# Merging two of the three products of a split-weight feed-forward, and spreading the conditioning steps

## Chip, core and metric

One NeuronCore of a Trainium2 chip runs the whole program; the other cores are idle. The metric is the device time of one execution in microseconds; for the kernel before, the median of three runs is 1975.13 us (1974.56 to 1978.75).

## What is computed

Two transformer blocks in a row, each of two layers, on one sequence of 256 tokens with 1024 features. All weights are fp32 and used once, so the program streams about 400 MB from HBM. The part that the change touches is the second block:

```python
cond = jax.nn.silu(c)
for l in range(DEPTH):                       # 2 layers
    mod = cond @ ada_w[l] + ada_b[l]         # 9 x 1024 values: the conditioning
    sh1, sc1, g1, sh2, sc2, g2, sh3, sc3, g3 = jnp.split(mod, N_MOD, axis=-1)
    hn = _modulate(_rms_norm(h, norm_g[l, 0]), sh1, sc1)
    h = h + 0.5 * g1[:, None, :] * _swiglu(hn, ffn1_w_in[l], ffn1_w_out[l])
    ...                                      # a mixer of four attention-like groups
    hn = _modulate(_rms_norm(h, norm_g[l, 2]), sh3, sc3)
    h = h + 0.5 * g3[:, None, :] * _swiglu(hn, ffn2_w_in[l], ffn2_w_out[l])

def _swiglu(x, w_in, w_out):                 # 1024 -> 2 x 2816 -> 1024
    gate, up = jnp.split(x @ w_in, 2, axis=-1)
    return (jax.nn.silu(gate) * up) @ w_out
```

So there are four feed-forwards, two in each layer of block 2. The conditioning is a vector times a 1024 x 9216 matrix per layer.

## The kernel before

Activations lie transposed: 128 features on the partitions, 256 tokens along the free axis, eight such tiles for 1024 features. A weight tile of 128 x 128 is the stationary operand of a TensorE product, and an activation tile of 256 columns moves past it.

**Three products per weight tile.** To keep fp32 accuracy with the fp32r format, each weight is split into a high part `wh` (a cast by ScalarE, L230) and a rest `wl` (a subtraction by VectorE, L231), and each activation into a high part `h` and a low part `l` (`hilo`, L201). `mm3` (L281) issues wh·h, wh·l and wl·h, 256 columns each, into one half of a PSUM bank; each product loads its own weights.

**Streaming.** `_plan` lists the weight chunks in order of use. `load_to` (L213) issues their DMAs on SyncE's queue, up to five sub-chunks of 128 x 1024 ahead; `split_to` (L222) splits up to three sub-chunks ahead, with four buffers each for `wh` and `wl`. `chunk` (L265) hands the tiles out and, at the start of every chunk, issues `prog["ada"]` conditioning steps. A chunk of the feed-forward is 8 x 256 columns: two sub-chunks, 16 weight tiles, 48 products.

**Conditioning.** `ada_step` (L530) does one of 144 steps: a 512 KB DMA into one of two buffers, and one VectorE multiply with a sum (L184, `ada<-ada,cond`) over 128 x 1024. `prog["ada"]` is set at L915 to L988 in block 1 and at L1082 and L1097 in `ffn`: 47 steps in each layer of block 1 (94), 24 in the first feed-forward, 26 in the second (two at each chunk from the third), none afterwards.

**Feed-forward** (`ffn`, L1065). The stage called f1 here (`gemm_shift`) multiplies the un-normalised input while the norm is computed. The stage f2 is 20 chunks; each gives one PSUM bank whose halves are gate and up. ScalarE reads the gate half and applies Silu (L1088), VectorE multiplies with the up half, and `hilo` splits the result into `hid`. The stage fd is the product with the second matrix: four groups of 256 output columns, each three chunks (8, 8 and 6 tiles deep), and after each group `gated_update` (L1049), two VectorE instructions that add the result to `x`. Names in the trace: tiles of f1 and f2 are `f`, those of fd `fd`; `hh`/`hl` and `hidh`/`hidl` are the two parts of an activation; `sg` and `sv` are the temporaries of the evacuation. Products carry L171 (`Bank.mm`), VectorE's helpers L184 to L193.

The tile framework's scheduler sets the order of the instructions on each engine's queue; every engine then works its queue in that order.

Of the kernel before, what the change touches and what calls it, by code (L numbers as in the profile page):

```python
# [121 lines left out]
def tile_model(ctx: ExitStack, tc: tile.TileContext, xT: bass.AP, pos: bass.AP, cvec: bass.AP, wst: bass.AP,  # L122
# [60 lines left out]
    def stt(out, in0, s, in1, op0, op1, **kw):  # L183
        nc.vector.scalar_tensor_tensor(out=out, in0=in0, scalar=s, in1=in1, op0=op0, op1=op1, **kw)  # L184

    def mul(out, a, b):
        tt(out=out, in0=a, in1=b, op=ALU.mult)

    def add(out, a, b):
        tt(out=out, in0=a, in1=b, op=ALU.add)  # L190
# [17 lines left out]
    for i, t in enumerate(subs):  # L208
        first_sub.setdefault(t[0], i)
    raws, split = {}, {}  # L210
    prog = {"raw": 0, "split": 0, "chunk": 0, "fill": 0, "turn": 0, "ada": 0}

    def load_to(s):  # L213
        while prog["raw"] < min(s, len(subs)):
# [50 lines left out]
    def chunk(key, l, k0, kk, c0, cc):  # L265
        j = prog["chunk"]
        assert plan[j] == (key, l, k0, kk, c0, cc), (plan[j], (key, l, k0, kk, c0, cc))
        prog["chunk"] += 1
        for _ in range(prog["ada"]):
            ada_step()  # L270
        s = first_sub[j]
        while s < len(subs) and subs[s][0] == j:
            split_to(s + 3)
            _, k, n, _, _ = subs[s]
            wh, wl = split.pop(s)
            for i in range(n):
                yield k0 + k + i, wh[:, i * cc:(i + 1) * cc], wl[:, i * cc:(i + 1) * cc]
            fill()
            s += 1
# [50 lines left out]
    def pair_outs(banks):  # L330
        return {m: (banks[m // 2], m % 2) for m in range(2 * len(banks))}
# [15 lines left out]
    def vc(n, i=0, k=1):  # L347
        return V[:, VC[n] + i:VC[n] + i + k]
# [24 lines left out]
    def sq_acc(j):  # L373
        t = t2("sq")
        act(t, xk(2 * j, 2), AF.Square)
        accumulate(0, j, t)

    class Act:
# [8 lines left out]

        def l(self, k, n=1):
            return self.lo[k // 4][:, (k % 4) * 256:(k % 4 + n) * 256]

    gfa = const([P, 8], "gfa")

# [137 lines left out]
    def ada_step():  # L530
        i = ada_n[1]
        if i >= L * 72:
            return
        ada_n[1] += 1
        ada_load(i + 2)
        l, j = i // 72, i % 72
        w = ada_raw.pop(i)
        stt(w, w, 1.0, cond[0], ALU.mult, ALU.mult, accum_out=mods[l][:, j:j + 1])
        if j == 71:
            add(mods[l], mods[l], vc(f"adab{l}", 0, 72))  # L540
            for q in range(3):
                stt(scl[l][:, 8 * q:8 * q + 8], mods[l][:, 24 * q + 8:24 * q + 16], 1.0, vc(f"ng{l}", 8 * q, 8),
                    ALU.add, ALU.mult)
                nc.vector.tensor_scalar_mul(hg[l][:, 8 * q:8 * q + 8], mods[l][:, 24 * q + 16:24 * q + 24],
                                            1.0 if q == 1 else 0.5)

    def ada_to(n):
        while ada_n[1] < n:
            ada_step()
# [69 lines left out]
    for l in range(L):  # L619
# [70 lines left out]
        def proj_pair(c, evac):  # L690
            b = Bank("pr", True)
            gemm([("A", l, 0, 8, c, 256)], h.h, h.l, pair_outs([b]), 7)
            evac(b)
# [210 lines left out]
        def gate_e(p):  # L904
            def f(b):
                s_ = th[p // 2][:, (p % 2) * 512:(p % 2) * 512 + 512]
                mul(v3(s_, 2), v3(b.t, 2), bc(rs, 2))
                if p % 4 == 3:
                    ins = act(th[p // 2], th[p // 2], AF.Tanh, scale=0.5)
                    with tc.issue_after(ins.ins):  # L910
                        ins = act(th[p // 2 - 1], th[p // 2 - 1], AF.Tanh, scale=0.5)
                    base_table(ins)
            return f

        prog["ada"] = 1  # L915
        for p in range(12):
            proj_pair(4352 + 256 * p, gate_e(p))

        prog["ada"] = 0
        mixed = [u4("mx") for _ in range(2)]  # L920
        mh = Act(8, "mh")
        for n, (y, gg) in enumerate(((ya, ga), (yb, gb), (yc, gc))):
# [45 lines left out]
        def hid_e(b, m):  # L968
# [3 lines left out]
            mul(q_, r_, r_)  # L972
            sub(hid.l(m, 2), q_, hid.h(m, 2).bitcast(F32))

        b4 = [Bank("u1", True) for _ in range(4)]
        gemm([("U", l, 2 * i, 2, 0, 1024) for i in range(4)], h.h, h.l, pair_outs(b4), 7, after={1: nrm2})
        for j in range(4):
# [2 lines left out]
        bd = [Bank("dn", True) for _ in range(4)]  # L980
        for half in range(2):
            for i in (range(4, 8) if half == 0 else range(8, 16)):
                prog["ada"] = min(2, i - 4)
                b = Bank("u2", half == 0)
                gemm([("U", l, 0, 8, 256 * i, 256)], h.h, h.l, pair_outs([b]), 7)
                hid_e(b, 2 * i)
            for m in range(4):
                prog["ada"] = 0 if half and m == 3 else 1  # L988
                gemm([("D", l, 8 * k, 8, 256 * m, 256) for k in (2 * half, 2 * half + 1)], hid.h, hid.l,
                     pair_outs([bd[m]]), 31)  # L990
                if half and l == 0:
                    update(m, bd[m], "full", rsm, "mix1", nh)
                elif half:
                    if m == 0:
                        ada_to(72)
                        mul(gfa, vc("final", 0, 8), scl[0][:, 0:8])
                        xa = Shifted(0, 0, lambda k: gfa[:, k:k + 1])
                    update(m, bd[m], "full", rsm)
                    xa.parts(m)
                    dst = t2("sqf")  # L1000
                    for e in range(2):
                        act(dst[:, e * 256:(e + 1) * 256], xk(2 * m + e), AF.Square, scale=vc("final", 2 * m + e))
                    accumulate(1, m, dst)
# [39 lines left out]
    def following(l, i):  # L1043
        l, i = (l, i + 1) if i < 2 else (l + 1, 0)
        if l == L:
            return None
        return Shifted(l, i, lambda k: scl[l][:, 8 * i + k:8 * i + k + 1])

    def gated_update(j, bank, l, i, nxt, part=None):  # L1049
        for e in range(2) if part is None else (part,):  # L1050
            k = 2 * j + e
            stt(xk(k), bank.t[:, e * 256:(e + 1) * 256], hg[l][:, 8 * i + k:8 * i + k + 1], xk(k), ALU.mult, ALU.add)
            if nxt is None:
                nc.sync.dma_start(outT[:, k * 256:(k + 1) * 256], xk(k))
        if nxt is None:
            return
        sq_acc(j)
        nxt.parts(j)

# [3 lines left out]
        return b  # L1063

    def ffn(l, f, i, xa, first=False):  # L1065
        h, r = Act(8, "h"), rcomb if first else rsx
        hid = Act(22, "hid")
        b4 = [Bank("f1", True) for _ in range(4)]
        nrm = normalised(h, l, i, first)
        gemm_shift(("F" + f, l, 0, 8, 0, 512), xa, b4, lambda: next(nrm))  # L1070
        for j in range(2):
            s_, q_ = t1("sg"), t1("sv")
            bg_, bu_ = b4[2 * j], b4[2 * j + 1]
            cg, cu = shift_bias(bg_), shift_bias(bu_)
            mul(s_, bg_.t[:, 0:256], r)
            act(s_, s_, AF.Silu, bias=cg)
            mul(q_, bu_.t[:, 0:256], r)
            stt(q_, q_, cu, s_, ALU.add, ALU.mult)
            hilo(q_, hid.h(j), hid.l(j))
        for j in range(20):  # L1080
            if j == 2:
                prog["ada"] = 1 if first else 2  # L1082
            if first and j in range(2, 10):
                next(nrm)
            b = Bank("f2", True)
            gemm([("F" + f, l, 0, 8, 512 + 256 * j, 256)], h.h, h.l, pair_outs([b]), 7)
            s_, q_ = t1("sg"), t1("sv")
            ins = act(s_, b.t[:, 0:256], AF.Silu)  # L1088
            mul(q_, s_, b.t[:, 256:512])
            hilo(q_, hid.h(j + 2), hid.l(j + 2))  # L1090
        if i == 2:
            ada_to(L * 72)
        nxt = following(l, i)
        base_table(ins)
        for m in range(4):
            if m == 2:
                prog["ada"] = 0  # L1097
            b = Bank("fd", True)
            parts = [("G" + f, l, k, kk, 256 * m, 256) for k, kk in ((0, 8), (8, 8), (16, 6))]
            if nxt is None and m == 3:  # L1100
                gemm(parts[:2], hid.h, hid.l, pair_outs([b]), 21)
                parts = list(chunk(*parts[2]))
                for e in range(2):
                    for k, wh, wl in parts:
                        mm3(b, b.t[:, e * 256:e * 256 + 256], wh[:, e * P:(e + 1) * P], wl[:, e * P:(e + 1) * P],
                            hid.h(k), hid.l(k), k == 21)
                    gated_update(m, b, l, i, nxt, e)
            else:
                gemm(parts, hid.h, hid.l, pair_outs([b]), 21)
                gated_update(m, b, l, i, nxt)  # L1110
        return nxt
# [411 lines left out]
```

## Time and profile before

| What | Value |
|---|---|
| median of 3 runs | 1975.13 us (1974.56 to 1978.75) |
| profiled execution, its own time | 1979.56 us |
| its span, first to last instruction | 1977.8 us |
| PE busy, DVE busy, ACT busy | 1950.8, 1465.2, 1084.9 us |
| products (MATMUL) | 15554 |
| HBM read | 402.96 MB, 204 GB/s over the span |
| mean granted TensorE clock | 0.991 |

The profiled execution lies 4.4 us above the median of the runs; the span is 1.8 us shorter than the execution. Products are pipelined: a product's duration in the trace (283 ns for 256 columns) is its latency, and what a stream of them costs is the distance from one start to the next.

### The profile page before, as it was taken

What the parts mean: (1) busy time and instruction counts of PE and PEld (TensorE: products, weight loads), DVE (VectorE), ACT (ScalarE), POOL (GpSimd) and SP (SyncE); (2) the same over time, 40 slices, a digit from 0 to 9 for tenths busy, and PEclk for the clock granted to TensorE, in tenths of its full rate; (3) what the DMA queues carried; (4) which work ended last, traced back from release to release, by engine and by line L of the source; (5) the groups of instructions that cost most, each with busy time, mean ns of one, the idle gap of its engine ahead of it and who ended that gap; (6) DMA issues with size and microseconds to landing.
All of it is one profiled execution on the core that took longest, in us unless ns stands there. A gap on an engine that the chain in (4) does not pass through costs nothing.

```text
span 1977.8 us, 38149 instructions
## 1 busy us (share of the span) xinstructions
PE 1950.8 (99%) x15554; PEld 1883.1 (95%) x15554; DVE 1465.2 (74%) x2243; ACT 1084.9 (55%) x1654; POOL 86.3 (4%) x86
## 2 busy tenths in 40 slices
PE   8999999999999999999999999999999999999999
PEld 7989999999999999999999997999999999889999
DVE  7878778696677786789877698788565557977553
ACT  5756545354565555445644467744464446576442
POOL 1000010001000010002000000000000000000000
PEclk9999999999999999999999998999999999999999
DMA  7545656896444655888577643388556555334554
GB/s 257 178 154 202 219 183 244 303 322 234 155 150 167 229 186 187 304 318 293 200 283 265 222 145 117 108 304 313 189 166 211 183 176 167 121 126 162 182 173 126
DMA packets 114945, 406.51 MB, mean 206 GB/s; under 512 B 12880, under 2 KB 14672, under 8 KB 114768
## 3 DMA queue, kind: packets, MB, share of 16 engines
q1 hardware_dynamic: 114768, 404.06, 59.8%
q8 instruction: 122, 2.00, 0.4%
q14 instruction: 55, 0.45, 0.1%
HBM read 402.96 MB, written 1.05 MB: 204 GB/s over the span
## 4 chain that ended last, share of the span: by engine, by line
PE 87%; DVE 6%; ACT 3%; DMA 2%; issue 1%; SPq 0%; POOL 0%; POOLq 0%; DVEq 0%; ACTq 0%
PE f L171 23%; PE fd L171 13%; PE pr L171 12%; PE dn L171 9%; PE u L171 9%; PE br L171 3%; PE wo L171 2%; PE mo L171 2%; DVE wl L231 2%; PE a L171 2%; DVE cv L184 1%; DMA raw<-wst_dram 1%; PE sbv L171 1%; PE rv L171 1%; PE uq L171 1%
## 5 line engine op out<-in xcount | busy, mean ns | idle before, releaser
L230 ACT CAST wh<-raw 128x1024 fp32r<-128x1024 f32 (+1 forms) x627 | 643.5, 1030 | 679.5 <-PE fd L171 119.8
L231 DVE TENSOR_TENSOR wl<-raw,wh 128x1024 fp32r<-128x1024 f32 (+1 forms) x627 | 756.0, 1210 | 330.0 <-ACT wh L230 329.0
L171 PE MATMUL f<-hh,wl 128*128 128x256 f32 x1280 | 363.8, 284 | 2.0 <-DVE wl L231 1.8
L171 PE MATMUL f<-hh,wh 128*128 128x256 f32 x1280 | 363.1, 284 | 0.8 <-ACT wh L230 0.8
L171 PE MATMUL f<-hl,wh 128*128 128x256 f32 x1280 | 363.0, 284 | 0.6 <-DVE hl L193 0.6
L171 PEld LDWEIGHTS f<-hh,wl 128*128 128x128 f32 x1280 | 246.4, 193 | 3.6 <-DVE wl L231 3.6
L171 PEld LDWEIGHTS f<-hh,wh 128*128 128x128 f32 x1280 | 246.4, 193 | 1.1 <-ACT wh L230 1.0
L171 PEld LDWEIGHTS f<-hl,wh 128*128 128x128 f32 x1280 | 246.4, 192 | 0.8 <-DVE hl L193 0.8
L184 DVE SCALAR_TENSOR_TENSOR ada<-ada,cond 128x1024 f32<-128x1024 f32 x144 | 176.5, 1227 | 59.5 <-DMA ada<-ada_dram 58.9
L171 PE MATMUL fd<-hidh,wh 128*128 128x256 f32 x704 | 199.3, 283 | 0.6 <-DVE x L184 0.6
L171 PE MATMUL fd<-hidl,wh 128*128 128x256 f32 x704 | 199.2, 283 | 0.0
L171 PE MATMUL fd<-hidh,wl 128*128 128x256 f32 x704 | 199.2, 283 | 0.0
L171 PE MATMUL pr<-hh,wh 128*128 128x256 f32 x672 | 194.8, 290 | 0.0
L171 PE MATMUL pr<-hl,wh 128*128 128x256 f32 x672 | 190.0, 283 | 0.0
L171 PE MATMUL pr<-hh,wl 128*128 128x256 f32 x672 | 190.0, 283 | 0.0
L171 PE MATMUL u<-hh,wh 128*128 128x256 f32 x512 | 145.3, 284 | 0.0
L171 PE MATMUL dn<-hidh,wh 128*128 128x256 f32 x512 | 144.9, 283 | 0.0
L171 PE MATMUL dn<-hidl,wh 128*128 128x256 f32 x512 | 144.9, 283 | 0.0
L171 PE MATMUL dn<-hidh,wl 128*128 128x256 f32 x512 | 144.9, 283 | 0.0
L171 PE MATMUL u<-hh,wl 128*128 128x256 f32 x512 | 144.9, 283 | 0.0
L171 PE MATMUL u<-hl,wh 128*128 128x256 f32 x512 | 144.9, 283 | 0.0
L171 PEld LDWEIGHTS fd<-hidh,wh 128*128 128x128 f32 x704 | 135.2, 192 | 0.8 <-DVE x L184 0.8
(476 smaller groups left out, 4478.1 us busy)
## 6 DMA issues: line engine op xcount, KB each, us to landing
raw<-wst_dram SPq DMA_DIRECT2D x599, 512.0 KB, 3.8
ada<-ada_dram SPq DMA_DIRECT2D x144, 512.0 KB, 5.1
raw<-wst_dram SPq DMA_DIRECT2D x22, 256.0 KB, 2.7
raw<-wst_dram SPq DMA_DIRECT2D x4, 390.0 KB, 3.0
R<-ret_dram SPq DMA_DIRECT2D x2, 512.0 KB, 7.6
out_dram<-x SPq DMA_DIRECT2D x8, 128.0 KB, 4.0
C<-cst_dram SPq DMA_DIRECT2D x1, 896.0 KB, 7.2
v<-vec_dram SPq DMA_DIRECT2D x2, 448.0 KB, 5.0
```

The costliest lines, as they stand in the source:

```text
L171: nc.tensor.matmul(out, lhsT=lhsT, rhs=rhs, start=grp not in self.open, stop=stop, skip_group_check=True)
L184: nc.vector.scalar_tensor_tensor(out=out, in0=in0, scalar=s, in1=in1, op0=op0, op1=op1, **kw)
L230: nc.scalar.copy(wh[:, :n * cc], src)
L231: ins = tt(out=wl[:, :n * cc], in0=src, in1=wh[:, :n * cc].bitcast(F32), op=ALU.subtract)
```

## The change

In the four feed-forwards the activation pair is laid out so that the high and low part of a tile stand in one buffer, 512 columns apart (`Pair`), and `hl(k)` is one operand of two strips of 256 columns. `gemm_ab` issues, for each weight tile, one product wh·(h and l) of 512 columns over a whole PSUM bank and one product wl·h of 256 columns into the bank's first half. An output tile of 128 x 256 so takes a whole bank, whose halves have to be added: in f2 by a ScalarE copy and a VectorE add for gate and for up, in fd (the first three of the four groups) by two updates of `x` instead of one. f1 and the fourth group of fd keep `mm3`. The conditioning steps are counted in fractions per chunk: 0.5 in the first up-projection chunks, 1 in the later stages of the first block, 0.7 in f2 and 1 in the first three groups of fd, until all 144 are done; each third of a layer's modulation vector is finished as soon as its 24 steps are.

```diff
-        for _ in range(prog["ada"]):
+        prog["due"] += prog["ada"]
+        while prog["due"] >= 1.0:
+            prog["due"] -= 1.0
             ada_step()
...
+    class Pair(Act):
+        def __init__(self, n, s):
+            self.t = [u4(s, dt=F32R) for _ in range((n + 1) // 2)]
+        def h(self, k, n=1):
+            return self.t[k // 2][:, (k % 2) * 256:(k % 2 + n) * 256]
+        def l(self, k, n=1):
+            return self.t[k // 2][:, 512 + (k % 2) * 256:512 + (k % 2 + n) * 256]
+        def hl(self, k):
+            return v3(self.t[k // 2], 2)[:, :, (k % 2) * 256:(k % 2) * 256 + 256]
+
+    def gemm_ab(chunks, a, banks, klast):
+        for c in chunks:
+            for k, wh, wl in chunk(*c):
+                for m, b in enumerate(banks):
+                    b.mm(v3(b.t, 2), wh[:, m * P:(m + 1) * P], a.hl(k), stop=False)
+                    b.mm(b.t[:, 0:256], wl[:, m * P:(m + 1) * P], a.h(k), stop=k == klast)
...
-        if j == 71:
-            add(mods[l], mods[l], vc(f"adab{l}", 0, 72))
...
+        if j % 24 == 23:
+            q = j // 24
+            mq = mods[l][:, 24 * q:24 * q + 24]
+            add(mq, mq, vc(f"adab{l}", 24 * q, 24))
...
+        prog["ada"] = 0.5
         b4 = [Bank("u1", True) for _ in range(4)]
...
-                prog["ada"] = min(2, i - 4)
+                prog["ada"] = 1
...
+    def gated_update_ab(j, banks, l, i, nxt):
+        for e in range(2):
+            k = 2 * j + e
+            for c in range(2):
+                stt(xk(k), banks[e].t[:, c * 256:(c + 1) * 256], hg[l][:, 8 * i + k:8 * i + k + 1], xk(k), ALU.mult,
+                    ALU.add)
...
     def ffn(l, f, i, xa, first=False):
-        h, r = Act(8, "h"), rcomb if first else rsx
-        hid = Act(22, "hid")
+        h, r = Pair(8, "h"), rcomb if first else rsx
+        hid = Pair(22, "hid")
...
         for j in range(20):
-            if j == 2:
-                prog["ada"] = 1 if first else 2
+            prog["ada"] = 0.7
...
-            b = Bank("f2", True)
-            gemm([("F" + f, l, 0, 8, 512 + 256 * j, 256)], h.h, h.l, pair_outs([b]), 7)
+            bb = [Bank("f2", True) for _ in range(2)]
+            gemm_ab([("F" + f, l, 0, 8, 512 + 256 * j, 256)], h, bb, 7)
             s_, q_ = t1("sg"), t1("sv")
-            ins = act(s_, b.t[:, 0:256], AF.Silu)
-            mul(q_, s_, b.t[:, 256:512])
+            for t_, b in zip((s_, q_), bb):
+                nc.scalar.copy(t_, b.t[:, 256:512])
+                add(t_, b.t[:, 0:256], t_)
+            ins = act(s_, s_, AF.Silu)
+            mul(q_, s_, q_)
             hilo(q_, hid.h(j + 2), hid.l(j + 2))
-        if i == 2:
-            ada_to(L * 72)
...
         for m in range(4):
-            if m == 2:
-                prog["ada"] = 0
+            prog["ada"] = 1 if m < 3 else 0
+            parts = [("G" + f, l, k, kk, 256 * m, 256) for k, kk in ((0, 8), (8, 8), (16, 6))]
+            if m < 3:
+                bb = [Bank("fd", True) for _ in range(2)]
+                gemm_ab(parts, hid, bb, 21)
+                gated_update_ab(m, bb, l, i, nxt)
+                continue
```

What the scheduler makes of it shows on three queues in f2 of the second feed-forward. TensorE before, from the last tile of one pair of sub-chunk buffers (`wh_15479`, `wl_15480`) to the first of the next; the chunk's bank is `f_2405`:

```order
L171 MATMUL f_2405_15543<-hh_14992,wh_15479 128x256
L171 MATMUL f_2405_15543<-hl_14994,wh_15479 128x256
L171 MATMUL f_2405_15543<-hh_14992,wl_15480 128x256
L171 MATMUL f_2405_15543<-hh_14993,wh_15509 128x256
L171 MATMUL f_2405_15543<-hl_14995,wh_15509 128x256
L171 MATMUL f_2405_15543<-hh_14993,wl_15510 128x256
```

Every weight tile makes three products of 256 columns. And now, over four weight tiles; the chunk has a bank for gate, `f_2477`, and one for up, `f_2478`:

```order
L171 MATMUL f_2477_15442<-h_14605,wh_15390 128x512
L171 MATMUL f_2477_15442<-h_14605,wl_15391 128x256
L171 MATMUL f_2478_15443<-h_14605,wh_15390 128x512
L171 MATMUL f_2478_15443<-h_14605,wl_15391 128x256
L171 MATMUL f_2477_15442<-h_14606,wh_15390 128x512
L171 MATMUL f_2477_15442<-h_14606,wl_15391 128x256
L171 MATMUL f_2478_15443<-h_14606,wh_15390 128x512
L171 MATMUL f_2478_15443<-h_14606,wl_15391 128x256
```

Two products of 256 columns have become one of 512, and the third stays. VectorE in the same stage, before: one chunk's evacuation and two conditioning steps (`wl_15656` is used two chunks after `f_2405`, `wl_15699` three chunks after it).

```order
L187 TENSOR_TENSOR sv_15611<-sg_15610,f_2405_15543 128x256
L231 TENSOR_TENSOR wl_15656<-raw_15507,wh_15655 128x1024
L193 TENSOR_TENSOR hidl_15003<-sv_15611,hidh_14997 128x256
L231 TENSOR_TENSOR wl_15699<-raw_15550,wh_15698 128x1024
L184 SCALAR_TENSOR_TENSOR ada_15617,mods_161<-ada_15617,cond_1820 128x1024
L184 SCALAR_TENSOR_TENSOR ada_15620,mods_161<-ada_15620,cond_1820 128x1024
```

Both splits and two conditioning steps stand behind the multiply that waits for the chunk's last product. And now, from a chunk that has a conditioning step ahead of it to the next chunk's first add (`wl_15531` is used two chunks after `f_2477`, `wl_15565` three chunks after it):

```order
L184 SCALAR_TENSOR_TENSOR ada_15503,mods_161<-ada_15503,cond_1820 128x1024
L190 TENSOR_TENSOR sg_15491<-f_2477_15442,sg_15491 128x256
L231 TENSOR_TENSOR wl_15531<-raw_15410,wh_15530 128x1024
L190 TENSOR_TENSOR sv_15492<-f_2478_15443,sv_15492 128x256
L187 TENSOR_TENSOR sv_15492<-sg_15491,sv_15492 128x256
L231 TENSOR_TENSOR wl_15565<-raw_15447,wh_15564 128x1024
L193 TENSOR_TENSOR hid_14615<-sv_15492,hid_14615 128x256
L190 TENSOR_TENSOR sg_15550<-f_2488_15501,sg_15550 128x256
```

The weight splits keep their lead in the queue; two adds came in, and at most one conditioning step stands in a chunk instead of two. ScalarE for the same chunk, now:

```order
L1128 COPY sg_15491<-f_2477_15442 128x256
L230 CAST wh_15530<-raw_15410 128x1024
L1128 COPY sv_15492<-f_2478_15443 128x256
L1130 ACTIVATE sg_15491<-sg_15491 128x256
L230 CAST wh_15564<-raw_15447 128x1024
L202 CAST hid_14615<-sv_15492 128x256
```

Two copies came in, and the two casts of weights stand between the steps of the evacuation. The conditioning steps on VectorE's queue are now 80 in block 1, 23 in the first feed-forward, 23 in the second and 18 in the third.

## Rows read from the trace of the kernel before

**Rows 1.** Page, head and parts 1 and 2: busy time, share, count; granted clock in tenths.
```profile
span 1977.8 us, 38149 instructions
...
PE 1950.8 (99%) x15554; PEld 1883.1 (95%) x15554; DVE 1465.2 (74%) x2243; ACT 1084.9 (55%) x1654; POOL 86.3 (4%) x86
...
PEclk9999999999999999999999998999999999999999
```
**Rows 2.** Page, part 4: chain that ended last, by engine and by line.
```profile
PE 87%; DVE 6%; ACT 3%; DMA 2%; issue 1%; SPq 0%; POOL 0%; POOLq 0%; DVEq 0%; ACTq 0%
PE f L171 23%; PE fd L171 13%; PE pr L171 12%; PE dn L171 9%; PE u L171 9%; PE br L171 3%; PE wo L171 2%; PE mo L171 2%; DVE wl L231 2%; PE a L171 2%; DVE cv L184 1%; DMA raw<-wst_dram 1%; PE sbv L171 1%; PE rv L171 1%; PE uq L171 1%
```
**Rows 3.** Chain in time, first feed-forward: start us, us, what, count.
```profile
966.68 109.45 PE f L171 x910
1076.13 61.81 PE fd L171 x515
```
**Rows 4.** PE timeline, first mixer, 512-column products: start us, us, what.
```profile
1210.61 0.39 PE L171 MATMUL mv<-wh,hh 128*128 128x512 f32 x1
...
1216.06 0.39 PE L171 MATMUL mv<-wh,hl 128*128 128x512 f32 x1
```
**Rows 5.** PE timeline, block 1, 512-column products just after an interruption.
```profile
66.40 0.40 PE L171 MATMUL sbv<-wh,hl 128*128 128x512 f32 x1
...
68.71 0.39 PE L171 MATMUL sbv<-wl,hh 128*128 128x512 f32 x1
```
**Rows 6.** Tile f, f2 of feed-forwards 1, 2, 3: count, ns, first and last start us.
```profile
L171 PE MATMUL f<-hh,wh x320: 280/283/386, 959.0 to 1075.6; 128*128 128x256 f32 x160
...
L171 PE MATMUL f<-hh,wh x320: 280/283/415, 1279.0 to 1399.2; 128*128 128x256 f32 x160
...
L171 PE MATMUL f<-hh,wh x320: 280/283/283, 1475.7 to 1590.8; 128*128 128x256 f32 x160
```
**Rows 7.** Windows: us, PE, PEld, DVE, ACT, POOL busy, clock, DMA share, GB/s.
```profile
1279.00:1399.50 120.50, 118.18 (x962) 116.96 (x961) 96.00 (x152) 58.26 (x90) 0.00 (x0) 0.99 0.81 282
1363.90:1367.30 3.40, 3.40 (x18) 3.40 (x18) 3.40 (x7) 0.89 (x2) 0.00 (x0) 0.50 0.85 304
1475.70:1591.20 115.50, 115.46 (x963) 115.26 (x962) 68.49 (x94) 58.37 (x90) 0.00 (x0) 1.00 0.54 181
```
**Rows 8.** Waits of DVE, 1279 to 1399.5 us.
```profile
DVE ada L184 <- DMA ada<-ada_dram: 8.5, 10, 2.0
```
**Rows 9.** Waits of PE, whole program: us in total, times, longest.
```profile
PE f L171 <- DVE wl L231: 1.8, 4, 0.8
```
**Rows 10.** Page, part 5: busy us, mean ns, idle before.
```profile
L230 ACT CAST wh<-raw 128x1024 fp32r<-128x1024 f32 (+1 forms) x627 | 643.5, 1030 | 679.5 <-PE fd L171 119.8
L231 DVE TENSOR_TENSOR wl<-raw,wh 128x1024 fp32r<-128x1024 f32 (+1 forms) x627 | 756.0, 1210 | 330.0 <-ACT wh L230 329.0
...
L184 DVE SCALAR_TENSOR_TENSOR ada<-ada,cond 128x1024 f32<-128x1024 f32 x144 | 176.5, 1227 | 59.5 <-DMA ada<-ada_dram 58.9
```
**Rows 11.** Tiles f, fd, hidl, vn: ns least/median/most, first and last start.
```profile
L1088 ACT ACTIVATE sg<-f x80: 368/380/386, 966.2 to 1911.0; 128x256 f32<-128x256 f32 x80
L187 DVE TENSOR_TENSOR sv<-sg,f x80: 410/414/417, 968.0 to 1912.3; 128x256 f32<-128x256 f32 x80
...
L193 DVE TENSOR_TENSOR hidl<-sv,hidh x88: 414/424/429, 964.3 to 1913.2; 128x256 fp32r<-128x256 f32 x88
...
L1303 ACT COPY vn<-gv x4: 368/380/392, 1189.5 to 1705.2; 128x256 f32<-128x256 f32 x4
...
L184 DVE SCALAR_TENSOR_TENSOR x<-fd,hg,x x32: 472/476/484, 1093.4 to 1974.3; 128x256 f32<-128x256 f32 x32
```
**Rows 12.** DVE and ACT timelines, f2 of feed-forward 3, one evacuation.
```profile
1502.26 0.42 DVE L193 TENSOR_TENSOR hidl<-sv,hidh 128x256 fp32r<-128x256 f32 x1 [0.47 <-ACT hidh L202]
1503.21 1.23 DVE L231 TENSOR_TENSOR wl<-raw,wh 128x1024 fp32r<-128x1024 f32 x1 [0.53 <-ACT wh L230]
...
1501.82 0.41 ACT L202 CAST hidh<-sv 128x256 fp32r<-128x256 f32 x1 [1.34 <-DVE sv L187]
```

More of the change, by code (lines that the diff above doesn't have):

```diff
@@ L210, in tile_model @@
     raws, split = {}, {}
-    prog = {"raw": 0, "split": 0, "chunk": 0, "fill": 0, "turn": 0, "ada": 0}
+    prog = {"raw": 0, "split": 0, "chunk": 0, "fill": 0, "turn": 0, "ada": 0.0, "due": 0.0}
     def load_to(s):
@@ L538, in ada_step @@
         stt(w, w, 1.0, cond[0], ALU.mult, ALU.mult, accum_out=mods[l][:, j:j + 1])
-        if j == 71:
-            add(mods[l], mods[l], vc(f"adab{l}", 0, 72))
[L541 to L545, printed above, removed]
+        if j % 24 == 23:
+            q = j // 24
+            mq = mods[l][:, 24 * q:24 * q + 24]
+            add(mq, mq, vc(f"adab{l}", 24 * q, 24))
+            stt(scl[l][:, 8 * q:8 * q + 8], mq[:, 8:16], 1.0, vc(f"ng{l}", 8 * q, 8), ALU.add, ALU.mult)
+            nc.vector.tensor_scalar_mul(hg[l][:, 8 * q:8 * q + 8], mq[:, 16:24], 1.0 if q == 1 else 0.5)
     def ada_to(n):
@@ L994, in tile_model @@
                     if m == 0:
-                        ada_to(72)
+                        ada_to(24)
                         mul(gfa, vc("final", 0, 8), scl[0][:, 0:8])
@@ L1046, in following @@
             return None
+        ada_to(72 * l + 24 * (i + 1))
         return Shifted(l, i, lambda k: scl[l][:, 8 * i + k:8 * i + k + 1])
@@ L1056, in gated_update, with take_up @@
             return
+        take_up(j, nxt)
+    def gated_update_ab(j, banks, l, i, nxt):
[4 more added lines that the diff above has]
+                    ALU.add)
+            if nxt is None:
+                nc.sync.dma_start(outT[:, k * 256:(k + 1) * 256], xk(k))
+        if nxt is not None:
+            take_up(j, nxt)
+    def take_up(j, nxt):
         sq_acc(j)
@@ L1095, in ffn @@
         for m in range(4):
-            if m == 2:
-                prog["ada"] = 0
+            prog["ada"] = 1 if m < 3 else 0
[5 more added lines that the diff above has]
+                continue
             b = Bank("fd", True)
-            parts = [("G" + f, l, k, kk, 256 * m, 256) for k, kk in ((0, 8), (8, 8), (16, 6))]
             if nxt is None and m == 3:
```

## The prediction, made before the run

> **What bounds the kernel now.** I read the page first, then the chain, then TensorE's timeline inside the feed-forwards. TensorE (PE) is busy 99% of the span at the full clock in nearly every slice [rows 1], and the chain runs through it for 87%, 36% in the feed-forwards' tiles f and fd alone [rows 2]. So a feed-forward costs what its stream of products costs. That is the distance between starts, not the 283 ns of a product: in the first feed-forward 515 fd products follow each other in 61.81 us, 120.02 ns each, with nothing between them [rows 3].
>
> A product of 512 columns is in the trace too, in the mixer: 24 steps from 1210.61 to 1216.06 us, 227.1 ns each [rows 4]. So 256 more columns cost 107.1 ns, and about 13 ns of a product does not depend on its columns. Two merged products save that part once. Just behind an interruption the same kind of product runs at 231 ns (10 steps in 2.31 us, [rows 5]).
>
> Then f2 of the feed-forwards side by side. The third takes 115.1 us from its first to its last wh·h product, the first 116.6, the second 120.2 [rows 6]. The second is the one with two conditioning steps per chunk: it moves 282 GB/s against 181, VectorE (DVE) is busy 96.0 us against 68.5 [rows 7], and DVE stands 8.5 us there waiting for conditioning DMAs [rows 8]. PE waits for weight splits [rows 9], and after those waits the granted clock is 0.50, the 1.2 GHz level, for 3.4 us [rows 7]. So 5.1 us of that stage are not products.
>
> **The products.** f2 has 20 chunks of 16 weight tiles, 320; three groups of fd have 3 x 22 x 2 = 132. Over four feed-forwards 1808 weight tiles change from three products to two. Before, a tile costs 3 x 120.02 = 360.06 ns; after, 227.1 + 120.02 = 347.1. Saved: 1808 x 12.9 = 23.4 us.
>
> No row shows a product whose moving operand is two strips, as `hl(k)` is. Bounds: 227.1 if the strips stream as one [rows 4], 240.04 if the second costs as much as a product of its own [rows 3], thus 23.4 us down to 0. I take 227.1: the feed-forward's stream is as unbroken as the mixer's. At the 231 of rows 5 it would be 1808 x 9.0 = 16.3 us; that is the low end of my own case. Below 227.1 I do not go, because those rows already hold one weight load per product.
>
> The Trainium skill speaks against this sum: "TensorE: Matmul & The Clock Gate", section "Back-to-back issue gap", gives the isolated gap as N / 2.4 + 2.5 ns, so a merged pair would save 2.5 ns, an estimate of 4.5 us over the 1808 tiles in place of 23.4. The trace does not agree: by that formula 256 columns cost 109 ns, and rows 3 have 120.02.
>
> **The evacuation.** f2 adds two ScalarE (ACT) copies (0.38 us by the nearest PSUM copy) and two DVE adds per chunk (0.41 us, the multiply that reads PSUM now) [rows 11]. A chunk now lasts 16 x 347.1 = 5.55 us on PE. DVE's own work in it: two splits at 1.21, four small operations at 0.41 and 0.7 steps at 1.23 [rows 10, 11], 2.42 + 1.64 + 0.86 = 4.92 us; 5.29 in a chunk with a step. ACT: two casts at 1.03, two copies, Silu and the split cast, about 0.4 each: 3.6 us. Both fit, but a queue is worked in order, so I lay the queues out from the end t = 0 of a chunk's products. ACT: copy to 0.38, cast to 1.41, copy to 1.79, Silu to 2.17; the second cast needs a buffer that PE leaves half a chunk later, at 2.78, and ends at 3.81, the split cast [rows 12] at 4.22. DVE: add to 0.79, split from 1.41 to 2.62, add to 3.03, multiply to 3.44, split from 3.81 to 5.02, subtract to 5.43, conditioning step to 6.66. The next chunk's copy is there at 5.55 + 0.38 = 5.93, so its add starts 0.7 us late, at 6.66. That does not pile up: its second split cannot start before that chunk's 3.81 anyway, and the operations ahead of it still end by then. The splits made here belong to the chunks two and three further on; the first is done at 2.6 and used at 5.55 + 2.78 = 8.3 us. So PE waits for neither: cost nothing, hidden by products. Without that lead every microsecond of lateness is PE's.
>
> At the start of a feed-forward the cover is thin: the normalisation is still in DVE's queue when f2 begins, and the first f2 loses about 1.5 us against the third [rows 6]. Two more adds there are at most 0.82 us in each of four, 3.3 us; at the other end nothing. I take 1 us, since most of the queue there is ACT's.
>
> The two extra updates of x (0.48 us each, [rows 11]) in three groups of fd lie under the next group's 15 us of products: nothing. Without that cover they would cost 4 x 3 x 0.95 = 11 us.
>
> **The conditioning steps.** Still 144. Block 1 has 80 instead of 94, the feed-forwards 23, 23, 18 and 0 instead of 24, 26, 0, 0. Each is 1.23 us of DVE and a 512 KB DMA on SP's queue, among the weight loads. In the second feed-forward at most one step per chunk asks for 1.05 + 0.7 x 0.52 = 1.41 MB in 5.55 us, 255 GB/s, where two asked for 2.10 MB in 5.76, 364 GB/s; 304 were moved in its worst stretch [rows 7]. So the DMA waits, the PE waits and the clock drop go: 5.1 us back, at least none. In fd a step per chunk asks for (1.05 + 0.52) / 5.55 = 283 GB/s, 315 in the short third chunk: about the measured flow, carried by the weights loaded ahead. In the third feed-forward 18 steps fall where DVE has room (68.5 of 115.5 us, [rows 7]). The few small instructions that now finish each third of a modulation vector: nothing, there are six lots of them.
>
> **The sum.** 23.4 + 5.1 - 1.0 = 27.5 us. The profiled execution takes 1979.56 us (span 1977.8) and would take 1952.1; it lies 4.4 us over the median of the runs, 1975.13, so for the median I forecast 1947.6 us. A measurement here can tell about 0.2%, 4 us, from no change.
>
> **Rivals.** *A: DVE is late now and then.* All feed-forwards with steps behave like the second one now, which loses 5.1 us over its 13 chunks with steps, 0.39 each; the 42 f2 chunks with a step would lose 16.4 us: 1964. For it: DVE is fuller than today, 4.92 of 5.55 us. Against it: that stage lost its time with DMA waits [rows 8], which the spreading takes away.
>
> *B: the merged product costs what two cost, 240.04 ns*, because a second strip starts anew. Then only the conditioning gains: 1947.6 + 23.4 = 1971. Against it: rows 4, though with one strip. The skill's 2.5 ns would land near this case, an estimate of 1966.5.
>
> *C: the handovers set the period, slower.* DVE has waits of 0.47 and 0.53 us for ACT inside one evacuation today [rows 12]. If they stay and the new add waits 0.38 for its copy, a chunk with a step takes 5.29 + 0.47 + 0.53 + 0.38 = 6.67 us, 1.12 over PE's 5.55; 42 of them cost 47 us: 1994.6. It ends slower than today as soon as such a chunk passes 5.55 + 27.5 / 42 = 6.20 us. For it: strict order on both queues. Against it: in the new order splits stand in the places where those waits were, and the lead of two chunks.
>
> **How the numbers follow.** Forecast 0.81, A 0.09, B 0.05, C 0.05. My own case runs from 16.3 + 2.5 - 3.3 = 15.5 us saved (half of the 5.1 kept) to 28.5; that is 1960 to 1946.6. The range takes in A at its upper end and the 2 to 4 us by which runs differ: 1943.5 to 1964.5. Faster: the forecast, A and half of B, which ends at the bound of 4 us, 0.925; the rest of B is no change, C slower. Rounded 0.92, 0.03 and 0.05.
>
> **What would show it.** In f2 and fd the starts should alternate in steps of 227 and 120 ns, and f2 should take about 111 us in the second to fourth feed-forward alike, 112 in the first. PE's waits for weight splits and the half clock at 1364 us should be gone, and the half clocks in the mixers stay. DVE should be busy about 102 us in an f2 with steps. It is wrong if the wide product steps at 235 ns or more, or if PE waits for `wl` in every chunk.

## The result, and the profile after

The changed kernel takes 1957.12 us (median of 4 runs, 1951.53 to 1960.48) against 1975.55 (4 runs, 1974.56 to 1978.75): a ratio of 0.9907, interval 0.9892 to 0.9922, so 18.4 us gained. The forecast was 1947.6 us, with 27.5 us gained; 1957.1 lies inside its range. The profiled execution is the slowest of the four.

The head of the page, its granted clock and its chain, to be read against [rows 1, 2]: there are 1808 products fewer (13746 instead of 15554), and TensorE (PE) is still the bound.

```profile
span 1958.6 us, 34892 instructions
...
PE 1932.8 (99%) x13746; PEld 1782.3 (91%) x13746; DVE 1531.2 (78%) x2431; ACT 1134.3 (58%) x1814; POOL 85.1 (4%) x86
...
PEclk9999999999999999999999999899999999999999
...
PE 88%; DVE 7%; ACT 3%; issue 1%; DMA 0%; POOL 0%; SPq 0%; POOLq 0%; DVEq 0%; ACTq 0%
```

Did the evacuation stay hidden? PE's waits in the whole program, for the feed-forwards' tile f:

```profile
PE f L171 <- DVE h L193: 0.9, 1, 0.9
```

There is one wait, at the start of a feed-forward (the kernel before has one of 0.6 us there); the wait for `wl` of [rows 9] is gone. The windows of f2 in feed-forwards 1 to 4, against [rows 7] (us, then PE, PEld, DVE, ACT, POOL busy, clock, DMA share, GB/s):

```profile
958.80:1073.40 114.60, 113.53 (x641) 97.90 (x641) 99.36 (x169) 71.73 (x131) 0.00 (x0) 1.00 0.72 250
1276.60:1389.70 113.10, 113.10 (x642) 98.09 (x641) 96.57 (x163) 71.25 (x129) 0.00 (x0) 1.00 0.72 250
1465.00:1576.20 111.20, 111.20 (x642) 96.97 (x641) 95.74 (x162) 70.94 (x129) 0.00 (x0) 1.00 0.73 254
1778.40:1891.60 113.20, 113.20 (x642) 97.98 (x641) 82.67 (x130) 69.15 (x126) 0.00 (x0) 1.00 0.57 185
```

The clock is full in all four, PE has no gap in the last three, VectorE (DVE) has 15 to 31 us left. Yet the third takes 111.2 us and the second and fourth take 2 us more, with as many products, no wait, and in the fourth less DVE work and less traffic. So the products themselves are spaced differently. PE's timeline in the second (start us, busy us, what), from one wide product to the one 30 weight tiles on:

```profile
1300.31 0.40 PE L171 MATMUL f<-h,wh 128*128 128x512 f32 x1
1300.56 0.28 PE L171 MATMUL f<-h,wl 128*128 128x256 f32 x1
1300.67 0.40 PE L171 MATMUL f<-h,wh 128*128 128x512 f32 x1
1300.91 0.28 PE L171 MATMUL f<-h,wl 128*128 128x256 f32 x1
...
1310.91 0.40 PE L171 MATMUL f<-h,wh 128*128 128x512 f32 x1
```

and the same in the third:

```profile
1500.32 0.39 PE L171 MATMUL f<-h,wh 128*128 128x512 f32 x1
1500.55 0.27 PE L171 MATMUL f<-h,wl 128*128 128x256 f32 x1
1500.66 0.40 PE L171 MATMUL f<-h,wh 128*128 128x512 f32 x1
1500.89 0.28 PE L171 MATMUL f<-h,wl 128*128 128x256 f32 x1
...
1510.72 0.39 PE L171 MATMUL f<-h,wh 128*128 128x512 f32 x1
```

10.60 us / 30 = 353.3 ns per weight tile, and 10.40 / 30 = 346.7. The slow rhythm repeats after three tiles: wide and narrow steps of 233 + 117, 241 + 120 and 236 + 113 ns. The fast one has wide steps of 231 to 233 ns and narrow ones of 112 to 118.

Neither rhythm changes in the middle of an undisturbed stream. In this trace f2 of the second to fourth feed-forward has one irregular place each, 4 to 6 us after its start; what is ahead of it may run in the other rhythm, and what is behind it keeps its rhythm to the end of the merged part of fd. The third feed-forward, which counts as fast, began slowly (x2 is two products in one row):

```profile
1465.00 0.39 PE L171 MATMUL f<-h,wh 128*128 128x512 f32 x1
...
1470.65 0.64 PE L171 MATMUL f<-h,wh 128*128 128x512 f32 x2
...
1471.54 0.40 PE L171 MATMUL f<-h,wh 128*128 128x512 f32 x1
```

The first 16 tiles took 5.65 us, 353.1 ns each; the next two took 0.89 us instead of 0.7, and from there the stream is fast. What the irregular place is stays open.

A feed-forward has 452 merged tiles, so the two rhythms lie 452 x 6.67 = 3.01 us apart; against the 360.0 ns of before one saves 3.01 us and the other 6.03. Here feed-forwards 1, 2 and 4 were slow and 3 was fast: 3 x 3.01 + 6.03 = 15.1 us.

### The profile page after: what moved, and what is told of

The parts are those of the page before. It is cut to its first block, busy times and chain, and to the rows that moved or that the text cites. A ratio compares the mean times of both kernels' runs of the same rounds, so it can differ in the third digit from the quotient of the medians.

```text
span 1958.6 us, 34892 instructions
## 1 busy us (share of the span) xinstructions
PE 1932.8 (99%) x13746; PEld 1782.3 (91%) x13746; DVE 1531.2 (78%) x2431; ACT 1134.3 (58%) x1814; POOL 85.1 (4%) x86
## 4 chain that ended last, share of the span: by engine, by line
PE 88%; DVE 7%; ACT 3%; issue 1%; DMA 0%; POOL 0%; SPq 0%; POOLq 0%; DVEq 0%; ACTq 0%
PE f L171 24%; PE fd L171 13%; PE pr L171 13%; PE dn L171 9%; PE u L171 9%; PE br L171 4%; PE wo L171 2%; PE mo L171 2%; DVE wl L231 2%; DVE cv L184 2%; PE a L171 2%; PE sbv L171 1%; PE rv L171 1%; PE uq L171 1%; PE z L171 1%
## 5 line engine op out<-in xcount | busy, mean ns | idle before, releaser
L171 PE MATMUL f<-h,wh 128*128 128x512 f32 x1280 | 450.3, 398 | 0.9 <-DVE h L193 0.9
L171 PE MATMUL f<-h,wl 128*128 128x256 f32 x1280 | 358.0, 280 | 0.1
L171 PEld LDWEIGHTS f<-h,wh 128*128 128x128 f32 x1280 | 240.1, 188 | 59.7 <-DVE h L193 1.3
L171 PE MATMUL fd<-hid,wh 128*128 128x512 f32 (+1 forms) x880 | 249.3, 352 | 0.6 <-DVE x L184 0.6
L171 PEld LDWEIGHTS f<-h,wl 128*128 128x128 f32 x1280 | 241.2, 189 | 1.3 <-DVE wl L231 1.3
L171 PE MATMUL fd<-hid,wl 128*128 128x256 f32 x704 | 197.6, 281 | 0.0
L171 PEld LDWEIGHTS fd<-hid,wh 128*128 128x128 f32 x880 | 154.0, 189 | 25.2 <-DVE x L184 0.8
L171 PEld LDWEIGHTS fd<-hid,wl 128*128 128x128 f32 x704 | 133.4, 189 | 0.0
L171 PEld LDWEIGHTS pr<-hh,wh 128*128 128x128 f32 x672 | 128.7, 191 | 3.7 <-issue 2.3
L171 PEld LDWEIGHTS pr<-hl,wh 128*128 128x128 f32 x672 | 128.8, 192 | 1.1 <-issue 1.0
```

The lines of the kernel that those rows point to most:

```text
L171: nc.tensor.matmul(out, lhsT=lhsT, rhs=rhs, start=grp not in self.open, stop=stop, skip_group_check=True)
```

## The experiments

**Three questions at once: which part brings the gain, does the rhythm stay at its places, what makes it.** The change once more; each half of the change alone; and the product stretches alone.

`after_again`: the change, unaltered.

> The changed kernel as it is, a second trace. In the first one a weight tile's pair of products costs 353.3 ns in feed-forwards 1, 2 and 4 and 346.7 in feed-forward 3, each value steady for over 140 us. Rhythm theory: these are two rhythms that the stream of products keeps up by itself, and what ran just ahead decides which; then a feed-forward can change its value from one execution to the next, and the time with it by about 452 tiles x 6.6 ns = 3.0 us each. Place theory (rival): the value hangs on where the buffers of a feed-forward lie; then the same three have 353.3 again and the third 346.7. Time by both 1951 to 1961 us.

`ada_only`: the kernel before, three products, with the conditioning steps spread as in the change.

```diff
-        for _ in range(prog["ada"]):
+        prog["due"] += prog["ada"]
+        while prog["due"] >= 1.0:
+            prog["due"] -= 1.0
             ada_step()
...
+            prog["ada"] = 0.7
...
+            prog["ada"] = 1 if m < 3 else 0
```

> The kernel before with the conditioning steps spread as in the change, and three products per weight tile as before. My sum gave the spreading 5.1 us: f2 of the second feed-forward falls from 120.2 to about 115.1 us, PE's waits there and the half clock at 1364 us go, the rest stays: about 1970.4 us, ratio 0.9974. Rival: the steps that moved into the third feed-forward and into fd cost there what they no longer cost in the second; then no change, 1975.

`ab_only`: the change with the steps placed as before.

```diff
-            prog["ada"] = 0.7
+            if j == 2:
+                prog["ada"] = 1 if first else 2
...
+        if i == 2:
+            ada_to(L * 72)
...
```

> The changed kernel with the conditioning steps placed as before the change. If the two parts of the change only add up, the products alone give what the trace of the change shows for them, three feed-forwards x 452 x 6.8 + one x 452 x 13.4 = 15.3 us: 1960 us, and f2 of the second feed-forward is 5 us longer than that of the fourth. Rival: with the two more adds VectorE can't carry two steps per chunk, 2.42 + 1.64 + 2.46 = 6.52 us against 5.6 of products, so 13 chunks lose about 0.9 us each, 12 us in that stage: 1967 us.

`micro`: no model, only stretches of 128 weight tiles on the same kinds of buffers, each opened by a wait of PE for DVE and then by a number of short products ("kicks"), so that a stretch meets its first product in another way.

```python
...
for p in range(NPAIR):      # order "ab", strips or one strip
    a(p)                    # wh, 512 columns
    c(p, p >= fin)          # wl, 256 columns
...
```

> No part of the model is computed: the output is the input x. One set of buffers, stretches of 128 tiles each behind a wait of PE for VectorE: alternating 512 and 256 columns (two strips) with 0, 1, 2, 3 and 5 products of 128 columns ahead; 512 alone; 256 alone; alternating with one strip of 512; 256 first; two wide then two narrow; four wide then four narrow; three of 256. Rhythm theory: the alternating stretches fall into two values, 353 and 347 ns per tile, by what is ahead of them, with one strip as with two; 512 alone settles at 227, 256 alone at 120, groups of four near 347. Place theory: all alternating stretches of two strips have one value. Strip theory (second rival): one strip costs 347 always, two strips 353.

Measured, the kernel before taking 1974.9 us beside them: `after_again` 1956.17 (ratio 0.9904, 0.9887 to 0.9921), `ada_only` 1976.0 (1.0002, 0.9988 to 1.0016), `ab_only` 1960.85 (0.9911, 0.9882 to 0.9940). The products alone bring about 14 of the 18.7 us, with intervals that overlap; spreading alone brings nothing that can be told, at most 2.4 us by its interval. So the gain comes from the products, and what the spreading adds to them is taken up below. f2 of the second and fourth feed-forward in `after_again` (count, ns least/median/most, first and last start):

```profile
L171 PE MATMUL f<-h,wh x320: 392/395/499, 1277.2 to 1388.0; 128*128 128x512 f32 x160
...
L171 PE MATMUL f<-h,wh x320: 387/398/403, 1776.4 to 1889.3; 128*128 128x512 f32 x160
```

The second, slow in the first trace of the same program, is now fast (110.8 us, against 353.3 x 319 = 112.7); the fourth is slow. So the rhythm is not tied to the place in the program or its buffers.

`micro` (740.09 us) gives the prices without the model, each a stretch of equal products (start, length to the last modelled end, count):

```profile
219.62 5.60 PE L54 MATMUL wide<-h,wh 128*128 128x512 f32 x24
...
246.74 4.48 PE L54 MATMUL nar<-h,wl 128*128 128x256 f32 x36
```

23 steps in 5.60 - 0.39 us are 226.5 ns, and this is the form with two strips; with one strip [rows 4] have 227.1. 35 steps in 4.48 - 0.28 us are 120.0. Rival B falls: a second strip costs nothing. Three narrow products per tile cost 360.0 ns, as in the kernel before. Alternated, wide and narrow products ran at 346.7 ns per tile behind no kick and at 353.3 behind 1, 2, 3 and 5; twice 346.7 with one strip; 353.3 both times when the narrow one came first. Wide, wide, narrow, narrow gave 348.3 both times it was run. Four wide and four narrow, expected near 347, gave 350.0 behind no kick and 350.8 behind two.

**Are the two strips the cause?** In `micro` one strip had been fast twice. `whole` stores both parts of an activation tile side by side, so that the moving operand is one strip of 512; `whole_ab_only` adds the old placing of the steps to that; `micro2` runs strips and one strip behind 0 to 5 kicks and behind 6 to 9 narrow products; `before_again` is the kernel before, traced once more.

```diff
...
         def hl(self, k):
-            return v3(self.t[k // 2], 2)[:, :, (k % 2) * 256:(k % 2) * 256 + 256]
+            return self.t[k // 2][:, (k % 2) * 512:(k % 2) * 512 + 512]
...
-                    b.mm(v3(b.t, 2), wh[:, m * P:(m + 1) * P], a.hl(k), stop=False)
+                    b.mm(b.t, wh[:, m * P:(m + 1) * P], a.hl(k), stop=False)
...
```

> The changed kernel with the high and low part of an activation tile side by side, so that the moving operand of the wide product is one strip of 512 columns. In the stretches measured by themselves one strip ran at 346.7 ns per tile twice out of two, two strips at 346.7 once and at 353.3 four times. If one strip keeps the stream in the faster rhythm, all four feed-forwards show 346.7: f2 near 111 us in each but the first (112.5), 1808 x 6.6 = 11.9 us less than a changed kernel with all four slow, 9 us less than the first trace: 1948 us, and less spread between executions than the 9 us of the change. Rival: one strip had luck twice; then the feed-forwards are mixed again and the time is that of the change, 1956.

> The same with the conditioning steps placed as before the change, two per chunk in the second feed-forward. With the rhythm out of play it tells what the spreading is worth beside the merged products. If VectorE can't carry two steps and two more adds, that f2 loses 5 us or more against the one of the run named whole, as it did in the trace of the products alone (117.7 against 113.1): 1953 us. Rival: the loss shows in profiled executions only, and the times of the two agree within 2 us.

> No part of the model is computed: the output is the input x. Stretches of 128 tiles, alternating 512 and 256 columns, two strips and one strip in turn on the same buffers, behind 0 to 5 products of 128 columns or 6 to 9 products of 256 columns. Strip theory in its weaker form: one strip always ends in the rhythm of 346.7 ns, two strips in either. Rival: both layouts show both values.

> The kernel before, a second trace. In the first one f2 of the second feed-forward took 120.2 us, 5.1 more than the third, and 37 us of the whole ran at half clock. The spreading alone brought nothing in the times, 1976.0 against 1974.9 us. Theory: the 5 us belong to that one execution, and a second trace shows less of them. Rival: they are there again, and the spreading pays as much elsewhere, in the third feed-forward and the mixers.

Measured, the kernel before taking 1974.91 us: `whole` 1951.13 us (0.9883, 0.9866 to 0.9899), `whole_ab_only` 1961.08 (0.9930, 0.9917 to 0.9944). `micro2` (984.42 us), two stretches with strips (`str`) and two with one strip (`one`), behind 0 and 1 kicks, each pair of lines the start and, 12 tiles on, the end of a measurement:

```profile
29.64 0.39 PE L53 MATMUL str<-h,wh 128*128 128x512 f32 x1
...
33.80 0.39 PE L53 MATMUL str<-h,wh 128*128 128x512 f32 x1
...
79.95 0.39 PE L53 MATMUL one<-h,wh 128*128 128x512 f32 x1
...
84.11 0.39 PE L53 MATMUL one<-h,wh 128*128 128x512 f32 x1
...
124.61 0.40 PE L53 MATMUL str<-h,wh 128*128 128x512 f32 x1
...
128.85 0.40 PE L53 MATMUL str<-h,wh 128*128 128x512 f32 x1
...
169.63 0.40 PE L53 MATMUL one<-h,wh 128*128 128x512 f32 x1
...
173.87 0.40 PE L53 MATMUL one<-h,wh 128*128 128x512 f32 x1
```

4.16 / 12 = 346.7 and 4.24 / 12 = 353.3, each with strips and with one strip. One strip was fast behind 0, 3 and 5 kicks and slow behind 1, 2 and 4; strips were slow behind 1 and 4 only. Behind 6 to 9 narrow products strips were fast once (6) and one strip was fast once (9). So the strips are not the cause. Nor does the number of kicks fix the rhythm: strips behind 2, 3 and 5 were slow in `micro` and fast here. In the trace of `whole` itself the first feed-forward is fast as far as the middle of fd, and the second to fourth are slow:

```profile
L171 PE MATMUL f<-h,wh x320: 387/398/458, 1271.5 to 1384.2; 128*128 128x512 f32 x160
```

112.7 us, as in the change. Why `whole` nonetheless has the lowest median here is open. Its interval overlaps the change's, and its runs had a high granted clock, a mean of 0.995 to 0.997 where those of the kernel `grouped` below have 0.993 to 0.995.

`before_again` (1973.52 us) tests the 5.1 us that the prediction saw lost to DMA waits in the second feed-forward. Its f2 there, and its window:

```profile
L171 PE MATMUL f<-hh,wh x320: 280/283/284, 1280.4 to 1395.8; 128*128 128x256 f32 x160
```

```profile
1280.40:1396.10 115.70, 115.66 (x962) 115.29 (x961) 95.77 (x152) 58.76 (x90) 0.00 (x0) 1.00 0.83 294
```

115.4 us against 120.2 in [rows 6], clock 1.00, PE with no gap, DVE as busy as in [rows 7]. DVE waits 5.2 us for conditioning there and PE loses nothing by it. So the loss was an incident of the one execution that the prediction read; how often it comes is not known.

With merged products it is another matter. `ab_only` in the same stretch, window and waits of PE:

```profile
1275.90:1393.60 117.70, 114.99 (x642) 97.59 (x641) 106.58 (x186) 70.75 (x129) 0.00 (x0) 1.00 0.81 289
```

```profile
PE f L171 <- DVE wl L231: 2.0, 4, 0.8
PE f L171 <- ACT wh L230: 0.6, 1, 0.6
```

Two steps per chunk beside the new adds make DVE 106.6 us busy of 117.7, and PE waits for splits: f2 takes 117.7 us where the change's first trace has 113.1, 4.6 more, although its rhythm changes about the places where PE waits and a fifth of its tiles ran fast. By whole times, spreading is worth 10 us in the form with one strip (1961.08 against 1951.13, intervals apart) and 4.7 in the form with strips (1960.85 against 1956.17, intervals overlapping). The stretch shows 2.7 us of the ten (f2 of `whole_ab_only` 115.7 us against 113.0). The granted clock goes with part of the rest (mean 0.993 to 0.997 over its runs, 0.995 to 0.997 over those of `whole`). In the traces it is lower in the two mixers (0.95 and 0.95, from 1150 to 1265 and from 1650 to 1770 us, against 0.97 and 0.99), where neither kernel has a conditioning step. So part of the ten may not be the spreading's at all; this is not settled.

**Can the order take the rhythm away?** `grouped` runs, for each activation tile, both wide products and then both narrow ones. `micro3` runs four orders (wide wide narrow narrow; wide narrow narrow wide; two wide, four narrow, two wide; eight and eight), each behind 0, 1, 2 and 4 kicks. `after_third` is the change a third time. `grouped_all` also merges the fourth group of fd where another feed-forward follows.

```diff
                 for m, b in enumerate(banks):
                     b.mm(v3(b.t, 2), wh[:, m * P:(m + 1) * P], a.hl(k), stop=False)
+                for m, b in enumerate(banks):
                     b.mm(b.t[:, 0:256], wl[:, m * P:(m + 1) * P], a.h(k), stop=k == klast)
```

```diff
-            if m < 3:
+            if m < 3 or nxt is not None:
                 bb = [Bank("fd", True) for _ in range(2)]
```

> The changed kernel with the four products of a gate and an up tile in the order wide, wide, narrow, narrow. Measured by itself this order gave one value behind two different beginnings, 348.3 ns per tile. If that holds in the kernel, all four feed-forwards show 348.3: f2 near 111.5 us in the second to fourth and 113 in the first, 1808 x 11.8 = 21.3 us less products than before: 1953.6 us by the median 1974.9, and 9 us less than a changed kernel with four slow feed-forwards. Rival: the steady value is disturbed in the kernel by the waits at each chunk and the time is that of the change, 1956.5.

> No part of the model is computed: the output is the input x. Stretches of 128 tiles behind 0, 1, 2 and 4 products of 128 columns, in four orders of wide (a) and narrow (b) products: aabb, abba, aabbbbaa and eight a then eight b. If long runs of equal products are what settles, eight and eight come closest to 226.7 + 120 = 346.7 whatever is ahead; abba and aabbbbaa have no value yet. Rival: every order has a fast and a slow rhythm, and none is free of what is ahead of it.

> The changed kernel as it is, beside the run named grouped_all on the same chip, and a third trace. By the rhythm theory each of its four feed-forwards shows 346.7 or 353.3 ns per tile, mostly the slow one as so far (5 of 8), and the time scatters by more than the grouped order does: median 1956, range 8 us or more. Rival: the slow value is tied to feed-forwards 1 and 4, which had it in both traces.

> The grouped order (wide, wide, narrow, narrow), also in the fourth group of fd in the first three feed-forwards: 3 x 44 tiles go from 360.1 to 348.3 ns, 1.6 us. But the two updates of x more that this adds (0.95 us) stand at the end of the feed-forward, where the next stage waits for x: about 1 us lost in each of three places. I expect 1952.9 - 1.6 + 2.0, no difference from the run named grouped by what can be measured, and 3 to 4 us under the change beside it. Rival: the updates are hidden by the next stage's own start and it is 1951.3.

`micro3` (779.7 us): the first and the second order ran at 348.3 ns per tile behind every one of the four openings, the third at 350.8, the last at 349.2. The first order, 8 tiles apart:

```profile
40.25 0.62 PE L51 MATMUL two<-h,wh 128*128 128x512 f32 x2
...
43.04 0.63 PE L51 MATMUL two<-h,wh 128*128 128x512 f32 x2
```

In the kernel, `grouped` (third feed-forward, 30 tiles apart):

```profile
1500.15 0.63 PE L171 MATMUL f<-h,wh 128*128 128x512 f32 x2
1500.62 0.40 PE L171 MATMUL f<-h,wl 128*128 128x256 f32 x2
...
1510.60 0.63 PE L171 MATMUL f<-h,wh 128*128 128x512 f32 x2
```

10.45 / 30 = 348.3 ns, and all four feed-forwards alike; its second f2:

```profile
L171 PE MATMUL f<-h,wh x320: 389/396/501, 1277.4 to 1388.6; 128*128 128x512 f32 x160
```

111.2 us. `grouped` takes 1952.9 us (1951.3 to 1955.15, the kernel before at 1972.51; 0.9895, 0.9874 to 0.9916), `after_third` 1956.56 (1951.14 to 1959.6, the kernel before at 1974.53; 0.9906, 0.9885 to 0.9927), `grouped_all` 1953.98 (beside `after_third`; 0.9893, 0.9870 to 0.9916). The order does in every feed-forward what it was to do. The runs of each grouped kernel lie within 4 us, those of the change within 9.0, 3.5 and 8.5 us, the three times that it was measured. That the median is lower than the change's (1957.1, 1956.2, 1956.6) is likely, not shown, since the intervals overlap. Merging the fourth group gives nothing that can be told.

In the trace of `after_third` it is the second feed-forward that is slow and the fourth that is fast:

```profile
L171 PE MATMUL f<-h,wh x320: 387/398/458, 1273.4 to 1386.1; 128*128 128x512 f32 x160
...
L171 PE MATMUL f<-h,wh x320: 392/395/403, 1772.0 to 1882.9; 128*128 128x512 f32 x160
```

Over three traces of the change 5 of 12 feed-forwards were fast: the first never, the third always, the second and the fourth now one and now the other.

## Why the prediction was right, and where it was off

**Faster, by the mechanism named: right.** Merging saves the part of a product that does not depend on its columns. `micro` measures it: 2 x 120.0 - 226.5 = 13.5 ns, against the 12.9 of the prediction. `ada_only` shows that the spreading brings nothing that can be told by itself.

**The products, 23.4 us: the step that failed is "after, 227.1 + 120.02 = 347.1".** Both prices are right for a stream of one kind, and their sum was carried over to an alternation, which no row of before shows. There the pair costs 346.7 ns, which is that sum, or 353.3, and which of the two comes could not be told ahead. Saved were 15.1 us in the first trace and 18.1 in each of the other two (two slow feed-forwards and two fast: 2 x 3.01 + 2 x 6.03); the value of 346.7 in all four would have saved 24.1. By the prediction's own sign, wrong if the wide product steps at 235 ns or more, the slow feed-forwards fail: their wide steps have a mean of 236.7 ns, those of the fast one 231.8. That f2 would take 111 us in the second to fourth alike failed too: 113.1, 111.2 and 113.2. The low end of the prediction, 16.3 at 231 ns, was the nearer value, by luck: the products of [rows 5] are all of one width, and no run ties their 231 ns to the alternation.

Of what the prediction quoted from the Trainium skill, "TensorE: Matmul & The Clock Gate", section "Back-to-back issue gap", its N / 2.4 + 2.5 ns would have given an estimate of 4.5 us. The runs side with the row: 13.5 ns per product saved in streams of one kind, 15.1 to 18.1 us in the kernel.

**The conditioning, 5.1 us: failed.** The step was "the DMA waits, the PE waits and the clock drop go: 5.1 us back", read from one execution. `before_again` has neither the PE waits nor the clock drop in that stage, and `ada_only` gains nothing that can be told. In the change the clock is at 1.00 there and PE's waits for `wl` are gone, as forecast, but a second trace of before has that too. DVE still waits 5.1 us for conditioning in the change's second f2, against 8.5 in [rows 8] and 5.2 in the second trace of before, and PE does not wait for DVE:

```profile
DVE ada L184 <- DMA ada<-ada_dram: 5.1, 7, 1.0
```

What the prediction did not say is that the merged products need the spreading: without it PE waits 2.6 us for splits in that stage in `ab_only`, and 1.5 in `whole_ab_only`.

**The start-up, -1.0: not seen.** The first f2 takes 114.6 us where 320 tiles of its rhythm are 113.1, 1.5 us over, the same 1.5 that it had over the third before the change.

**The evacuation, nothing: right.** PE has one wait of 0.9 us for tile f in the whole program. DVE is busy 96.6 and 95.7 us in the f2 with steps (forecast about 102), which falls short of the 113 and 111 that PE needs. Rivals A and C fall with that, B with `micro`.

**The sum.** The products give 15.1, 18.1 and 18.1 us in the three traces, and the other two terms nothing; the medians measured are 18.4, 18.7 and 18.0 us below the kernel before. A trace is one execution and a median is several, so they need not agree closer. That the time fell inside the range is in part luck: at the low end of the prediction's own case, 16.3 + 2.5 - 3.3, two terms that were not there nearly cancel. In the profiled pair, 1979.56 - 1960.48 = 19.1, the products gave 15.1; the rest fits the 4.8 us incident of the trace of before (15.1 + 4.8 = 19.9, 0.8 too much).

## What to carry to other kernels

Take the price of a product from a stream with the same neighbours: prices from streams of one width added up in one rhythm of the alternation and not in the other, and two wide followed by two narrow cost the same every time. A loss that shows in one traced execution is a term of the sum only after a second trace shows it too. Removing products shortens the time that hid other work, so look at what else must then be thinned out: spreading the conditioning was worth nothing that can be told before. With the merged products the traces show 2.7 and 4.6 us for it in the second feed-forward, and the medians 4.7 and 10.

## What was not expected of the hardware

An alternation of 512- and 256-column products has two rhythms at the full granted clock, 346.7 and 353.3 ns per pair; each sustains itself over hundreds of products, and changes were seen only at an interruption or an irregular step. Which one starts differed between executions of the same program and behind different products ahead of the stream. One strip or two makes no difference. The two orders in pairs have one value, 348.3 ns, between the two. What inside the engine makes the slow one was not tried.

Executions of the kernel before lie up to 12 us apart, roughly in step with the mean granted clock: of its eleven runs beside `after_third`, the fastest took 1969.4 us at 0.998 and the slowest 1981.5 at 0.991. With merged products the clock alone does not order them: the fastest and the slowest run of `ab_only`, 1948.39 and 1962.79 us, had 0.998 and 0.997. The two rhythms would allow up to 12 us there (four feed-forwards of 3.0), but the run at 1948.39 was not traced. One profiled execution is a draw from that.
